# 128x128 squares transposed as two 64-row tiles into two PSUM banks, and scores times values spread over four quarters of TensorE

## The chip, the cores and the metric

The kernel runs on one core of one Trainium2 chip. A core has a matrix engine (TensorE, PE in the profile, with its weight loads listed apart as PEld), VectorE (DVE), ScalarE (ACT), GpSimd (POOL) and SyncE (SP), which here issues the DMAs. The metric is the device time of one execution in microseconds, as the median of several runs of the same program; lower is better.

## The reference, cut to what matters

The kernel computes one encoder block on 16 meta tokens and 1024 tokens of width 1024, all in float32.

```python
h = concat(meta, x)
u = rmsnorm(h)
a, q, k, v, r, lr, ga, gb = split(u @ w_in)
y_a = (pool(a) @ w_pool_mix * pool_scale) @ w_pool_out
# chunks of 64 tokens, 4 heads with keys of 64 and values of 128, b = cumsum(log decay) in a chunk
scores = sum_k q[t,k] * k[s,k] * exp(-|b[t,k] - b[s,k]|)
o  = scores @ v + (q * exp(b)) @ S
S  = exp(b_end) * S + (k * exp(b_end - b)).T @ v
y_b = (rmsnorm(o) * silu(r)) @ w_gla_out
h  = h + (sigmoid(ga) * y_a + sigmoid(gb) * y_b) @ w_out
h  = h + square(relu(rmsnorm(h) @ w_ff1)) @ w_ff2
return rmsnorm(h)[16:]
```

## The kernel before

Features lie on partitions and tokens along the free axis for every product that contracts over the width, so the normalised rows (tokens on partitions) must be transposed first. Every large product is done three times: each operand is split into a high part and a low part (a copy on ScalarE in the type `fp32r`, and a subtraction on VectorE), and `mm3` (L285, L286, L287) issues high×high, high×low and low×high into one accumulation. The two products of the MLP are each one level of a seven-product recursion on halves: `P1` to `P7` for the first (`ff1`), seven products over stored operands for the second (`ff2`).

The stages follow one another: `first` (rows normalised, turned by `turn` at L525, value projection at L285 to L287 in the bank `mm`), the remaining projections, the scores inside chunks (`scores`, L1188), the passes over chunk states (`across`, once for each half of the tokens and each pair `p` of heads), the merge of the two branches (`yb_block`, L1388 to L1393), the output projection (`out_tile`, once for eight tiles of 128 tokens and both column halves; its result leaves PSUM at L1572), the second normalisation with its transposes (`turn_tile`, L1589), then `ff1` and `ff2`.

What sets the order: TensorE's instructions stand in the order in which the program's steps emit them (a manual schedule for that engine). The instructions of ScalarE and VectorE are put in order by a scheduler. Every engine takes its own list strictly in order, and waits at an instruction until the semaphores that it names are there.

PSUM has eight banks of 128 partitions x 512 floats. `banks(keep, tag=n, ...)` closes pools down to `keep` and opens new ones: a tag has `n` buffers used in turn, of one bank each, or of two banks each for the tags that are asked for through `two` (the pairs `sc`, `gs`, `m2`). A buffer that is used again waits for the readers of its former content; a newly opened pool lies over old banks, so its first use of a bank waits for the last readers of what lay there. The pools named in the text are: at the start `sc=1, mm=3, ms=3`; in the passes over states `mm=3, m2=1, ms=1`; from the merge to the second normalisation `mm` kept at 3 and `ms=3`; in most of `ff1` `y=4, z=2` (opened in `ff_room`, `z` for the products P5 and P3).

A square is a 128x128 block of float32 that `pe.transpose` turns: the block is loaded as weights, and `ident`, the unit matrix, is moved through. There are 176: 64 in `first` (eight tiles of tokens, `turn(t, j)` does four squares for j = 0 and four for j = 1, alternating between a bank of `ms` and one of `sc`), 48 in `across` (L1417 turns the decayed keys `kl` into `kt`, L1461 turns the normalised output `on`), 64 in `turn_tile`. In `first`, a turned group of four is read by ScalarE (`keep`, L531, into `xr`; `hi`, L538, into `th`) and VectorE (`lo`, L541, into `tl`). In `turn_tile`, tiles 4 to 7 are read by ScalarE and VectorE to form sums and differences with the tile four before (L1599 to L1605) for the recursion. The last two tiles, 6 and 7, are turned between the first products of `ff1`.

In `across`, the parts of TensorE work on tiles of 64x64 at a `tile_position` (first row, first column of the tile in the array): `kt` times values (L1423) and the queries times states (L1447) use the four quarters in the order (0,0), (1,1), (1,0), (0,1). Scores times values (L1437) uses only the two on the diagonal. The result `o` holds for each head `e` a bank, with the two chunks `u` of a pair on the lower and the upper 64 partitions.

Of the kernel before, what the change touches and what calls it, by code (L numbers as in the profile page):

```python
# [122 lines left out]
def kernel(  # L123
# [25 lines left out]

    banks(sc=1, mm=3, ms=3)  # L150

# [108 lines left out]

    turn_n = [0]

    def transposed(u, half, at, tags=("ms",), to=None):
        rows = u.shape[0]
        th, tl = (t[half] for t in to or (TH, TL))
        if rows == P:
            for j in range(2):
                turn_n[0] += 1
                b = bank(tags[turn_n[0] % len(tags)]).rearrange("p (a b) -> p a b", a=4)
                for i in range(4):  # L270
                    pe.transpose(b[:, i], u[:, (4 * j + i) * P : (4 * j + i + 1) * P], ident)
                split_from_psum(th[:, 4 * j : 4 * j + 4, at : at + P], tl[:, 4 * j : 4 * j + 4, at : at + P], b)
                c = half * HALF + at - OFF[half]
                act.activation(S["xr"][:, 4 * j : 4 * j + 4, c : c + P], b, ACT.Copy)
        else:
            b = bank("ms")[:, : 8 * rows].rearrange("p (a b) -> p a b", a=8)
            for i in range(8):
                pe.transpose(b[:, i], u[:, i * P : (i + 1) * P], ident[:rows, :rows])
            split_from_psum(th[:, :, at : at + rows], tl[:, :, at : at + rows], b)

# [164 lines left out]
    def first_stage(xs, us, xm, um, lrraw):  # L445
# [75 lines left out]
        def turn(t, j):  # L521
            turn_n[0] += 1
            b = turned[t, j] = bank(("ms", "sc")[turn_n[0] % 2]).rearrange("p (a b) -> p a b", a=4)
            for i in range(4):
                pe.transpose(b[:, i], x_out(t)[:, (4 * j + i) * P : (4 * j + i + 1) * P], ident)  # L525

        def kept(t, j):
            return xr[:, 4 * j : 4 * j + 4, t * P : (t + 1) * P]

# [3 lines left out]
        def part(a, t, j):  # L533
            half, at = tok(t)
            return a[half][:, 4 * j : 4 * j + 4, at : at + P]

# [65 lines left out]
    def quad(a):  # L602
        return a.rearrange("p (k c) -> p k c", k=4)
# [571 lines left out]

    def part(i):
        return slice(i * CH, (i + 1) * CH)

    def scores(kk, qq):


        turn_n[0] += 1
        c = (turn_n[0] % 2) * 4 * CH
        b = two("gs")[:, :, c : c + 4 * CH].rearrange("p e (j t) -> p e j t", j=4)
        for j in range(4):
            for e, u in ((0, 0), (1, 1), (1, 0), (0, 1)):
                r, to, s = part(e), part(u), part(2 * j + u)
                pe.matmul(b[to, e, j], kk[r, s], qq[r, s], start=True, stop=True, tile_position=(e * CH, u * CH))  # L1188
        return b
# [90 lines left out]
    def gla_open():  # L1280
# [16 lines left out]
        for half in range(2):  # L1297
# [3 lines left out]
            if half == 0:  # L1301
                ask(6)
        banks(keep=1, mm=3, m2=1, ms=1)

# [99 lines left out]
    def across(p, half):  # L1404
# [9 lines left out]
        sr = S["sr"][p].rearrange("p e t -> p (e t)")  # L1414
        b = quad(bank("ms") if p == 0 else wide2()[:, 0])
        for j in range(4):
            pe.transpose(b[:, j], kl[:, j * P : (j + 1) * P], ident)  # L1417
        act.activation(kt, b, ACT.Copy)
        yield 1.4
        kv = wide2().rearrange("p u (j c) -> p u j c", j=4)  # L1420
        for j in range(4):
            for u, e in ((0, 0), (1, 1), (1, 0), (0, 1)):
                pe.matmul(  # L1423
                    kv[part(e), u, j], kt[part(u), j, part(e)], v[part(u), j, e], start=True, stop=True,
                    tile_position=(u * CH, e * CH),
                )
# [7 lines left out]
        for j in range(4):  # L1434
            for e in range(2):
                for u in range(2):
                    pe.matmul(  # L1437
                        o[part(u), e, j], scc[part(u), e, j], v[part(u), j, e], start=j == 0, stop=False,
                        tile_position=(u * CH, u * CH), skip_group_check=True,
                    )  # L1440

        dve.tensor_copy(rms[p][:, :2], o[:, :, 3, P - 1])
        yield 0.8
        for j in (3, 0, 1, 2):
            for e, u in ((0, 0), (1, 1), (1, 0), (0, 1)):
                c = 2 * j + u
                pe.matmul(  # L1447
                    o[part(u), e, j], qe[part(e), part(c)], states[c][part(e)], start=False, stop=True,
                    tile_position=(e * CH, u * CH), skip_group_check=True,
                )  # L1450
# [7 lines left out]
        yield 8.0  # L1458
        b = wide2().rearrange("p e (j c) -> p (e j) c", j=4)
        for j in range(8):  # L1460
            pe.transpose(b[:, j], on[:, j], ident)  # L1461
        dve.tensor_tensor(sr, b.rearrange("p a c -> p (a c)"), sr, ALU.mult)
        yh, yl = (S["yg"][half][:, n, 2 * p : 2 * p + 2].rearrange("p e t -> p (e t)") for n in range(2))
# [42 lines left out]
    def merge_open():  # L1506
        banks(keep=2, ms=3)
        left.pop_to(left_m)
# [69 lines left out]

    def turn_tile(t, tags=("ms",)):

        u, acc, g = S["u2"][:, ORDER.index(t) % 2], S["acc"], t % 4
        cols, b = slice(g * P, (g + 1) * P), []
        for j in range(2):
            turn_n[0] += 1
            b.append(quad(bank(tags[turn_n[0] % len(tags)])))
            for i in range(4):
                pe.transpose(b[j][:, i], u[:, (4 * j + i) * P : (4 * j + i + 1) * P], ident)  # L1589
        lo, hi = (quad(acc[:, g, c]) for c in halves())  # L1590
        if t < 4:
            for j, raw_copy in enumerate((lo, hi)):
                k = slice(4 * j, 4 * j + 4)
                act.activation(raw_copy, b[j], ACT.Copy)
                split_from_psum(MH[0][:, k, cols], ML[0][:, k, cols], b[j])
# [3 lines left out]
        dve.tensor_tensor(t1, b[0], lo, ALU.subtract)  # L1599
        act.activation(MH[1][:, 0:4, cols], t1, ACT.Copy)  # L1600
        dve.tensor_tensor(ML[1][:, 0:4, cols], t1, f32(MH[1][:, 0:4, cols]), ALU.subtract)  # L1601
        split_from_psum(MH[1][:, 4:8, cols], ML[1][:, 4:8, cols], b[1])
        dve.tensor_tensor(lo, b[1], t1, ALU.subtract)
        dve.tensor_tensor(b12, b[1], b12, ALU.subtract)
        dve.tensor_tensor(hi, hi, lo, ALU.subtract)  # L1605
# [267 lines left out]
    def ff_layers():  # L1873
# [58 lines left out]
```

## Time and profile before

| quantity | value |
|---|---|
| median of 3 runs | 1202.58 us (1202.22 to 1203.32) |
| profiled execution | 1203.16 us |
| span in its profile (first to last instruction) | 1201.4 us |
| TensorE busy | 1187.1 us, 99% of the span |
| VectorE, ScalarE, GpSimd busy | 854.1, 578.7, 101.5 us |
| mean granted TensorE clock | 0.998 |
| 128x128 transposes | 176 matmuls of some 272 ns each, overlapped in the array |

A row of the timeline gives the start in us from the beginning of the span, a duration, the engine, the line, the operation, output<-inputs, and how many records stand together in it; `128*128` is the weight tile and `128x128` the output. TensorE overlaps its matmuls, so how fast it goes is read from the distance between starts, not from the durations. In brackets behind a row stands how long the engine was idle before it and which instruction ended that. A table of stretches (windows) gives the busy time of each engine in each stretch.

### The profile page before, as it was taken

What the parts mean: (1) busy time and instruction counts of PE and PEld (TensorE: products, weight loads), DVE (VectorE), ACT (ScalarE), POOL (GpSimd) and SP (SyncE); (2) the same over time, 40 slices, a digit from 0 to 9 for tenths busy, and PEclk for the clock granted to TensorE, in tenths of its full rate; (3) what the DMA queues carried; (4) which work ended last, traced back from release to release, by engine and by line L of the source; (5) the groups of instructions that cost most, each with busy time, mean ns of one, the idle gap of its engine ahead of it and who ended that gap; (6) DMA issues with size and microseconds to landing.
All of it is one profiled execution on the core that took longest, in us unless ns stands there. A gap on an engine that the chain in (4) does not pass through costs nothing.

```text
span 1201.4 us, 18340 instructions
## 1 busy us (share of the span) xinstructions
PE 1187.1 (99%) x6775; PEld 987.7 (82%) x6775; DVE 854.1 (71%) x1392; ACT 578.7 (48%) x1006; POOL 101.5 (8%) x121
## 2 busy tenths in 40 slices
PE   9999999999999999999999999999999999999997
PEld 7999888777778887888788888888888888888886
DVE  6679557575676669617886767667675887887686
ACT  7566544444455224205754545545454444445554
POOL 0224232333220000000000000000000000000000
PEclk9999999999999999999999999999999999999999
DMA  8232633434358877801264444444389963333532
GB/s 246 68 89 80 182 109 119 144 117 141 124 178 269 304 229 269 268 26 71 88 198 136 158 147 162 148 158 161 128 282 324 336 222 97 97 97 92 172 97 88
DMA packets 151001, 192.79 MB, mean 160 GB/s; under 512 B 12088, under 2 KB 85616, under 8 KB 150912
## 3 DMA queue, kind: packets, MB, share of 16 engines
q1 hardware_dynamic: 150752, 191.56, 49.6%
q8 instruction: 53, 0.87, 0.3%
q14 instruction: 36, 0.29, 0.1%
q10 hardware_dynamic: 160, 0.07, 0.0%
HBM read 128.66 MB, written 62.93 MB: 159 GB/s over the span
## 4 chain that ended last, share of the span: by engine, by line
PE 68%; DVE 3%; issue 1%; DMA 1%; ACT 1%; SPq 0%; DVEq 0%
PE b_oa L287 5%; PE b_oa L286 5%; PE b_oa L285 5%; PE b_y L285 4%; PE b_y L287 4%; PE b_y L286 4%; PE b_mm L285 4%; PE b_mm L287 4%; PE b_mm L286 4%; PE b_ob L287 4%; PE b_ob L286 4%; PE b_ob L285 4%; PE b_z L286 3%; PE b_z L285 3%; PE b_z L287 3%; PE b_sc L285 2%
## 5 line engine op out<-in xcount | busy, mean ns | idle before, releaser
L285 PE MATMUL b_z<-th,w1h 128*128 128x512 f32 x240 | 94.3, 393 | 0.0
L286 PE MATMUL b_z<-tl,w1h 128*128 128x512 f32 x240 | 93.5, 390 | 0.4 <-DVE tl L1601 0.4
L287 PE MATMUL b_z<-th,w1l 128*128 128x512 f32 x240 | 93.5, 390 | 0.0
L285 PE MATMUL b_sc<-th,w1h 128*128 128x512 f32 (+1 forms) x232 | 89.8, 387 | 0.6 <-ACT u2p L1715 0.6
L286 PE MATMUL b_sc<-tl,w1h 128*128 128x512 f32 (+1 forms) x232 | 89.2, 385 | 0.0
L967 ACT ACTIVATE w1h<-raw 128x512 fp32r<-128x512 f32 x103 | 64.0, 622 | 52.4 <-PE b_y L286 23.0
L287 PE MATMUL b_sc<-th,w1l 128*128 128x512 f32 (+1 forms) x232 | 88.9, 383 | 0.0
L967 ACT ACTIVATE w1h<-fs 128x512 fp32r<-128x512 f32 x81 | 51.1, 631 | 66.3 <-PE b_y L286 34.8
L968 DVE TENSOR_TENSOR w1l<-raw,w1h 128x512 fp32r<-128x512 f32 x103 | 70.7, 688 | 15.7 <-ACT w1h L967 15.7
L968 DVE TENSOR_TENSOR w1l<-fs,w1h 128x512 fp32r<-128x512 f32 x81 | 56.2, 693 | 21.6 <-ACT w1h L967 21.6
L967 ACT ACTIVATE w1h<-bt 128x512 fp32r<-128x512 f32 x46 | 29.1, 632 | 70.9 <-issue 43.9
L1791 DVE TENSOR_TENSOR bt<-w,w 128x512 f32<-128x512 f32 x80 | 54.8, 684 | 1.1 <-DMA w<-in_w_ff_dram 1.1
L286 PEld LDWEIGHTS b_z<-tl,w1h 128*128 128x128 f32 x240 | 45.1, 188 | 9.9 <-DVE tl L1601 0.8
L285 PEld LDWEIGHTS b_z<-th,w1h 128*128 128x128 f32 x240 | 45.0, 188 | 9.8 <-issue 0.3
L287 PEld LDWEIGHTS b_z<-th,w1l 128*128 128x128 f32 x240 | 45.1, 188 | 9.7
L285 PEld LDWEIGHTS b_sc<-th,w1h 128*128 128x128 f32 x232 | 43.5, 188 | 10.3 <-ACT u2p L1715 1.1
L287 PEld LDWEIGHTS b_sc<-th,w1l 128*128 128x128 f32 x232 | 43.6, 188 | 8.9
L286 PEld LDWEIGHTS b_sc<-tl,w1h 128*128 128x128 f32 x232 | 43.6, 188 | 8.6
L285 PE MATMUL b_mm<-wo,th 128*128 128x512 f32 x128 | 50.4, 393 | 0.0
L968 DVE TENSOR_TENSOR w1l<-bt,w1h 128x512 fp32r<-128x512 f32 x46 | 31.8, 691 | 25.6 <-ACT w1h L967 25.6
L287 PE MATMUL b_mm<-wo,tl 128*128 128x512 f32 x128 | 49.9, 390 | 0.0
L286 PE MATMUL b_mm<-wo,th 128*128 128x512 f32 x128 | 49.8, 389 | 0.0
(526 smaller groups left out, 3416.3 us busy)
## 6 DMA issues: line engine op xcount, KB each, us to landing
hf_dram<-h SPq DMA_DIRECT2D x112, 256.0 KB, 2.1
raw<-hf_dram SPq DMA_DIRECT2D x112, 256.0 KB, 2.7
w<-in_w_ff_dram SPq DMA_DIRECT2D x64, 256.0 KB, 4.8
raw<-in_w_in_dram SPq DMA_DIRECT2D x18, 512.0 KB, 4.7
raw<-in_w_ff_dram SPq DMA_DIRECT2D x16, 512.0 KB, 4.3
rawx<-in_w_ff_dram SPq DMA_DIRECT2D x16, 512.0 KB, 4.1
rawp<-in_w_in_dram SPq DMA_DIRECT2D x14, 512.0 KB, 4.7
xs<-in_x_dram SPq DMA_DIRECT2D x8, 512.0 KB, 5.2
```

The source lines that it names most:

```text
L285: pe.matmul(ps, ah, bh, start=first and i == 0, stop=False, skip_group_check=more)
L286: pe.matmul(ps, ah, bl, start=False, stop=False, skip_group_check=more)
L287: pe.matmul(ps, al, bh, start=False, stop=last and i == n - 1, skip_group_check=more)
L967: act.activation(hi, a, ACT.Copy)
L968: dve.tensor_tensor(lo, a, f32(hi), ALU.subtract)
L1791: dve.tensor_tensor(bt, w, S["w2"][q[3:]][:, i], ALU.add if q[2] == "+" else ALU.subtract)
```

## The change

`turn_square` replaces one transpose of 128 rows by two transposes of 64 rows: rows 0 to 63 at `tile_position` (0, 0) into the first bank of a pair, rows 64 to 127 at (64, 0) into the second bank, each with 64 columns of `ident`. A square so takes two weight loads of 64x128 and two matmuls of 64 columns, where it took one load of 128x128 and one matmul of 128 columns. 176 loads and 176 matmuls become 352 each. The readers see the pair through `turned_view`, as blocks of 2 x 64 columns. All eight squares of a tile lie in one pair (`sc` and the new `y2` in turn in `first`, `m2` or `sc` in `across`, `m2` in `turn_tile`), so the readers of either group of four lie on the same pair.

In scores times values the second head `e = u ^ to` of each chunk goes to the other half of the rows of the result, so that the product uses all four quarters. The result's halves are swapped for that head, and after the turning L1462's one operation of VectorE becomes three, which swap them back.

To make room for the pairs, the PSUM pools change: at the start `mm=3, ms=1`, with the pair `y2`; in the passes over states `mm=4, m2=1` with no `ms`; in the merge `mm` stays at 4 and `m2=1`; at `wo1_open`, a new set `mm=2, m2=2`.

```diff
-    banks(sc=1, mm=3, ms=3)
+    banks(sc=1, mm=3, ms=1, y2=1)
+    QUARTERS = ((0, 0), (1, 1), (1, 0), (0, 1))
+    def turn_square(pair, k, a):
+        for u in range(2):
+            pe.transpose(pair[:, u, part(k)], a[part(u)], ident[part(u), part(u)], tile_position=(u * CH, 0))
+    def turned_view(pair, n):
+        return pair.rearrange("p u (k s) -> p k u s", s=CH)[:, n]
+    def four(a):
+        return a.rearrange("p k (u s) -> p k u s", s=CH)
...
         def turn(t, j):
-            turn_n[0] += 1
-            b = turned[t, j] = bank(("ms", "sc")[turn_n[0] % 2]).rearrange("p (a b) -> p a b", a=4)
-            for i in range(4):
-                pe.transpose(b[:, i], x_out(t)[:, (4 * j + i) * P : (4 * j + i + 1) * P], ident)
+            if j == 0:
+                turned[t] = two("y2" if t % 2 else "sc")
+            for k in range(4 * j, 4 * j + 4):
+                turn_square(turned[t], k, x_out(t)[:, k * P : (k + 1) * P])
+            turned[t, j] = turned_view(turned[t], slice(4 * j, 4 * j + 4))
...
-        banks(keep=1, mm=3, m2=1, ms=1)
+        banks(keep=1, mm=4, m2=1)
...
-        b = quad(bank("ms") if p == 0 else wide2()[:, 0])
+        b = wide2()
         for j in range(4):
-            pe.transpose(b[:, j], kl[:, j * P : (j + 1) * P], ident)
-        act.activation(kt, b, ACT.Copy)
+            turn_square(b, j, kl[:, j * P : (j + 1) * P])
+        act.activation(four(kt), turned_view(b, slice(0, 4)), ACT.Copy)
...
         for j in range(4):
-            for e in range(2):
-                for u in range(2):
-                    pe.matmul(
-                        o[part(u), e, j], scc[part(u), e, j], v[part(u), j, e], start=j == 0, stop=False,
-                        tile_position=(u * CH, u * CH), skip_group_check=True,
-                    )
+            for u, to in QUARTERS:
+                e = u ^ to
+                pe.matmul(
+                    o[part(to), e, j], scc[part(u), e, j], v[part(u), j, e], start=j == 0, stop=False,
+                    tile_position=(u * CH, to * CH), skip_group_check=True,
+                )
...
-        b = wide2().rearrange("p e (j c) -> p (e j) c", j=4)
+        b = wide2()
         for j in range(8):
-            pe.transpose(b[:, j], on[:, j], ident)
-        dve.tensor_tensor(sr, b.rearrange("p a c -> p (a c)"), sr, ALU.mult)
+            turn_square(b, j, on[:, j])
+        sr8 = four(sr.rearrange("p (a c) -> p a c", c=P))
+        turned = turned_view(b, slice(0, 8))
+        dve.tensor_tensor(sr8[:, :4], turned[:, :4], sr8[:, :4], ALU.mult)
+        for u in range(2):
+            dve.tensor_tensor(sr8[:, 4:, u], turned[:, 4:, 1 - u], sr8[:, 4:, u], ALU.mult)
...
     def merge_open():
-        banks(keep=2, ms=3)
+        banks(keep=2, m2=1)
...
     def wo1_open():
         raw.back()
+        banks(keep=1, mm=2, m2=2)
...
-    def turn_tile(t, tags=("ms",)):
+    def turn_tile(t):
...
+        cols, b, pair = slice(g * P, (g + 1) * P), [], two("m2")
         for j in range(2):
-            turn_n[0] += 1
-            b.append(quad(bank(tags[turn_n[0] % len(tags)])))
-            for i in range(4):
-                pe.transpose(b[j][:, i], u[:, (4 * j + i) * P : (4 * j + i + 1) * P], ident)
+            k = slice(4 * j, 4 * j + 4)
+            for i in range(4 * j, 4 * j + 4):
+                turn_square(pair, i, u[:, i * P : (i + 1) * P])
+            b.append(turned_view(pair, k))
...
-        b12, t1 = (quad(acc[:, t, c]) for c in halves())
-        act.activation(b12, b[0], ACT.Copy)
-        dve.tensor_tensor(t1, b[0], lo, ALU.subtract)
+        b12, t1 = (quad(acc[:, t, c]) for c in halves())
+        act.activation(four(b12), b[0], ACT.Copy)
+        dve.tensor_tensor(four(t1), b[0], four(lo), ALU.subtract)
...
-                turn_tile(ORDER[6 + n // 2], ("mm", "ms"))
+                turn_tile(ORDER[6 + n // 2])
```

The program after is some lines longer: in its listings L525, L1417, L1461 and L1589 are all L270, mm3 is L290 to L292, L1572 is L1580, L1538 is L1545, L1599, L1601, L1603, L1604 are L1606, L1608, L1610, L1611, and L1003, L1669 are L1009, L1676.

First place: TensorE in `first`, about the turning of tile 3, which stands between products of the value projection. Before (`us` is the normalised tile, `vw` the weights):

```order
L287 MATMUL b_mm<-vw_186,tl_136 128x256
L525 MATMUL b_sc<-ident,us 128x128 x4
L525 MATMUL b_ms<-ident,us 128x128 x4
L285 MATMUL b_mm<-vw_186,th_132 128x256
L286 MATMUL b_mm<-vw_186,th_132 128x256
```

and after:

```order
L292 MATMUL b_mm<-vw_189,tl_139 128x256
L270 MATMUL b_y_392<-ident,us 128x64 x16
L290 MATMUL b_mm<-vw_189,th_135 128x256
L291 MATMUL b_mm<-vw_189,th_135 128x256
L292 MATMUL b_mm<-vw_189,tl_139 128x256
```

The block stands at the same place; its eight matmuls into two banks, which came free one by one, are sixteen into the pair `y2` that tile 1 had used.

Second place: VectorE at the opening of the output projection's second part. Before (L1538 makes the low part of the second half of `w_out`, L1572 moves `out_tile`'s result out of PSUM, L968 makes the low parts of the first weights of `ff1`):

```order
L1393 SCALAR_TENSOR_TENSOR tl_144<-o,th_140 128x512
L1538 TENSOR_TENSOR wo_4966<-raw_116,wo_4966 128x1024
L1538 TENSOR_TENSOR wo_4966<-rawx_4962,wo_4966 128x1024
L1572 TENSOR_TENSOR acc<-b_mm,acc 128x512
L1538 TENSOR_TENSOR wo_4966<-raw_120,wo_4966 128x1024
L968 TENSOR_TENSOR w1l<-raw_116,w1h 128x512 x2
L1572 TENSOR_TENSOR acc<-b_mm,acc 128x512
```

and after:

```order
L1396 SCALAR_TENSOR_TENSOR tl_147<-o,th_143 128x512
L1545 TENSOR_TENSOR wo_5090<-raw_119,wo_5090 128x1024
L1545 TENSOR_TENSOR wo_5090<-raw_123,wo_5090 128x1024
L1580 TENSOR_TENSOR acc<-b_mm,acc 128x512
L1545 TENSOR_TENSOR wo_5090<-rawx_5086,wo_5090 128x1024
L974 TENSOR_TENSOR w1l<-raw_119,w1h 128x512 x2
L1580 TENSOR_TENSOR acc<-b_mm,acc 128x512
```

The first L1572 (now L1580) empties the bank of `out_tile(1, 0)` and stands behind two splits of `w_out` in both; the second split is now of `raw_123` instead of `rawx`. What is new is who waits for it: the pool `mm=2` that `wo1_open` opens lies over that bank, so the next tile, `out_tile(2, 0)`, starts behind it.

Third place: VectorE where tile 7 is turned and `ff1` goes on with its first product P5. Before (L968 is a low part of weights, L1609 the low part of a sum):

```order
L968 TENSOR_TENSOR w1l<-fs,w1h 128x512
L1599 TENSOR_TENSOR acc<-b_ms,acc 128x512
L222 TENSOR_TENSOR tl_144<-b_mm,th_140 128x4x128
L1603 TENSOR_TENSOR acc<-b_mm,acc 128x512
L1601 TENSOR_TENSOR tl_144<-acc,th_140 128x4x128
L1604 TENSOR_TENSOR acc<-b_mm,acc 128x512
L1605 TENSOR_TENSOR acc<-acc 128x512
```

and after:

```order
L974 TENSOR_TENSOR w1l<-fs,w1h 128x512
L1606 TENSOR_TENSOR acc<-b_m_5799,acc 128x512
L1009 TENSOR_TENSOR fs<-fs,raw_119 128x512
L1676 TENSOR_TENSOR t4l<-acc,t4h 128x4x128
L1608 TENSOR_TENSOR tl_147<-acc,th_143 128x4x128
L222 TENSOR_TENSOR tl_147<-b_m_5799,th_143 128x4x128
L1610 TENSOR_TENSOR acc<-b_m_5799,acc 128x512
L1611 TENSOR_TENSOR acc<-b_m_5799,acc 128x512
L1612 TENSOR_TENSOR acc<-acc 128x512
```

P5's first matmul waited for the ScalarE half of the split at L222 and its second for L1601. After, its first matmul waits for L1611 too, since the bank `z` that it writes lies over the pair of tile 7, and L1009 and L1676 have come ahead of that.

More of the change, by code (lines that the diff above doesn't have):

```diff
@@ L261, with part, transposed @@
     turn_n = [0]
-    def transposed(u, half, at, tags=("ms",), to=None):
+    QUARTERS = ((0, 0), (1, 1), (1, 0), (0, 1))
+    def part(i):
+        return slice(i * CH, (i + 1) * CH)
+    def turn_square(pair, k, a):
[5 more added lines that the diff above has]
+        return a.rearrange("p k (u s) -> p k u s", s=CH)
+    def transposed(u, half, at, to=None):
         rows = u.shape[0]
         th, tl = (t[half] for t in to or (TH, TL))
-        if rows == P:
-            for j in range(2):
-                turn_n[0] += 1
-                b = bank(tags[turn_n[0] % len(tags)]).rearrange("p (a b) -> p a b", a=4)
-                for i in range(4):
[L271 to L279, printed above, removed]
+        b = bank("ms")[:, : 8 * rows].rearrange("p (a b) -> p a b", a=8)
+        for i in range(8):
+            pe.transpose(b[:, i], u[:, i * P : (i + 1) * P], ident[:rows, :rows])
+        split_from_psum(th[:, :, at : at + rows], tl[:, :, at : at + rows], b)
     def mm3(ps, n, lhs, rhs, first=True, last=True, more=False):
@@ L521, in turn @@
         def turn(t, j):
[L522 to L525 removed]
+            if j == 0:
[3 more added lines that the diff above has]
+            turned[t, j] = turned_view(turned[t], slice(4 * j, 4 * j + 4))
         def kept(t, j):
[L528 removed]
+            return four(xr[:, 4 * j : 4 * j + 4, t * P : (t + 1) * P])
         def keep(t, j):
@@ L534, in part @@
             half, at = tok(t)
-            return a[half][:, 4 * j : 4 * j + 4, at : at + P]
+            return four(a[half][:, 4 * j : 4 * j + 4, at : at + P])
         def hi(t, j):
@@ L1185, in scores @@
         for j in range(4):
-            for e, u in ((0, 0), (1, 1), (1, 0), (0, 1)):
+            for e, u in QUARTERS:
                 r, to, s = part(e), part(u), part(2 * j + u)
@@ L1421, in across @@
         for j in range(4):
-            for u, e in ((0, 0), (1, 1), (1, 0), (0, 1)):
+            for u, e in QUARTERS:
                 pe.matmul(
@@ L1444, in across @@
         for j in (3, 0, 1, 2):
-            for e, u in ((0, 0), (1, 1), (1, 0), (0, 1)):
-                c = 2 * j + u
+            for e, to in QUARTERS:
+                c = 2 * j + (to ^ e)
                 pe.matmul(
-                    o[part(u), e, j], qe[part(e), part(c)], states[c][part(e)], start=False, stop=True,
-                    tile_position=(e * CH, u * CH), skip_group_check=True,
+                    o[part(to), e, j], qe[part(e), part(c)], states[c][part(e)], start=False, stop=True,
+                    tile_position=(e * CH, to * CH), skip_group_check=True,
                 )
@@ L1577, in out_tile @@
         return fn
-    def turn_tile(t, tags=("ms",)):
+    def turn_tile(t):
         u, acc, g = S["u2"][:, ORDER.index(t) % 2], S["acc"], t % 4
-        cols, b = slice(g * P, (g + 1) * P), []
+        cols, b, pair = slice(g * P, (g + 1) * P), [], two("m2")
         for j in range(2):
-            turn_n[0] += 1
-            b.append(quad(bank(tags[turn_n[0] % len(tags)])))
-            for i in range(4):
-                pe.transpose(b[j][:, i], u[:, (4 * j + i) * P : (4 * j + i + 1) * P], ident)
+            k = slice(4 * j, 4 * j + 4)
+            for i in range(4 * j, 4 * j + 4):
+                turn_square(pair, i, u[:, i * P : (i + 1) * P])
+            b.append(turned_view(pair, k))
+        at = lambda a, k=slice(0, 4): four(a[:, k, cols])
         lo, hi = (quad(acc[:, g, c]) for c in halves())
```

12 lines of the change are left out of this document (5 added, 7 removed).

## The prediction

> **What bounds the kernel now.** I read the page's head, the slices and the chain that ended last first, then the stretches, then the places that the change touches row by row.
>
> ```profile
> PE 1187.1 (99%) x6775; PEld 987.7 (82%) x6775; DVE 854.1 (71%) x1392; ACT 578.7 (48%) x1006; POOL 101.5 (8%) x121
> ```
>
> TensorE is busy for all but 14.3 us of 1201.4 us. A nanosecond saved on TensorE is a nanosecond of the total, as long as no other engine is late at that place. Where that fails shows in the stretches (columns: length, PE, PEld, DVE, ACT, POOL busy, clock, DMA share, GB/s):
>
> ```profile
> 10.00:20.00 10.00, 9.54 (x65) 8.46 (x65) 8.72 (x18) 8.37 (x18) 0.00 (x0) 1.00 0.91 265
> 460.00:500.00 40.00, 39.12 (x172) 31.99 (x173) 32.49 (x46) 15.60 (x21) 0.00 (x0) 1.00 0.91 315
> 580.00:600.00 20.00, 18.93 (x89) 15.14 (x88) 18.89 (x34) 14.02 (x27) 0.00 (x0) 1.00 0.25 79
> ```
>
> The granted clock is full. Before 20 us TensorE waits for others and ScalarE and VectorE are busy for over 8 of 10 us, at 460 to 500 us transfers are at 91%, and at 580 to 600 us VectorE is busy for 18.89 of 20. The change frees TensorE mostly elsewhere, but it also alters waits in three of these four stretches.
>
> **What a square costs, before and after.** Before: L1461's sixteen squares of one block, between ordinary matmuls.
>
> ```profile
> 414.44 1.03 PE L1461 MATMUL b_m<-ident,on 128*128 128x128 f32 x8
> 415.31 1.04 PE L1461 MATMUL b_sc<-ident,on 128*128 128x128 f32 x8
> 416.10 0.48 PE L285 MATMUL b_mm<-th,w1h 128*128 128x512 f32 x1
> ```
>
> Eight squares take 415.31 − 414.44 = 0.87 us, 109 ns each, and nothing is lost on entering the block. After, a square is two weight loads of 64x128 and two matmuls of 64 columns at two row positions. No row has just that form; two come near.
>
> ```profile
> 330.67 0.39 PE L287 MATMUL b_y<-t1h,w1l 128*128 128x512 f32 x1
> ...
> 331.51 0.24 PE L1188 MATMUL b_gs<-n 64*64 64x64 f32 x4
> 331.51 0.66 PE L1188 MATMUL b_gs<-n 64*64 64x64 f32 x32
> ...
> 332.43 0.39 PE L286 MATMUL b_z<-tl,w1h 128*128 128x512 f32 x1
> ...
> 55.98 0.26 PEld L278 LDWEIGHTS b_ms<-ident,um 16*128 16x128 f32 x3 [0.15 <-DVE lrtok L406]
> 55.98 0.57 PEld L278 LDWEIGHTS b_ms<-ident,um 16*128 16x128 f32 x8 [0.15 <-DVE lrtok L406]
> ```
>
> The scores move 64 columns through four tiles of 64x64. Their second 32 matmuls, seen first as far as the first four go and then whole, last 0.24 and 0.66 us: seven more groups of four in 0.42 us, 60 ns a group. So four loads and four matmuls of 64 columns, at both row positions and into both banks, share 60 ns. L278 turns the meta rows (16 rows) with loads of full 128 columns: three last 0.26 us and eight 0.57, five more in 0.31, 62 ns each. So I price a new square at 60 to 62 ns instead of 109.
>
> The block of scores also pays for being in tiles. From the last ordinary start ahead of it to the second one behind it are 332.43 − 330.67 = 1.76 us; two ordinary spacings of 0.23 and sixteen groups of 60 ns make 1.42, so 0.34 us is entering and leaving. I take 0.30 to 0.36. A block of eight squares before takes 8 × 109 = 0.88 us; after, 8 × (60 to 62) + (0.30 to 0.36) = 0.78 to 0.86 us, so 0.02 to 0.10 us is won. The one block of sixteen (L1461, first half) wins about 0.4 us. There are 21 blocks: 8 in the first stage, 5 in the passes over states, 8 in the normalisation. Twenty blocks of eight give 0.4 to 2.0 us and the large one 0.4; the first three, in the fed stretch, and the last two, which the wait described below swallows, count for little. I take **−1.4 us**, range −2.4 to −0.6.
>
> [...]
>
> **Scores times values.** Two quarters before, four after; the nearest row is `kt` times values, the same tile, columns and count on four quarters.
>
> ```profile
> 387.30 1.10 PE L1423 MATMUL b_m<-v,kt 64*64 64x128 f32 x32
> 388.22 1.05 PE L1423 MATMUL b_sc<-v,kt 64*64 64x128 f32 x32
> 389.21 0.50 PE L285 MATMUL b_mm<-th,w1h 128*128 128x512 f32 x1
> ...
> 396.27 1.96 PE L1437 MATMUL b_m<-v,gi 64*64 64x128 f32 x32
> 398.07 1.91 PE L1437 MATMUL b_sc<-v,gi 64*64 64x128 f32 x32
> 399.91 0.50 PE L285 MATMUL b_mm<-th,w1h 128*128 128x512 f32 x1
> ```
>
> One block: 399.91 − 396.27 = 3.64 us against 389.21 − 387.30 = 1.91 us, so 1.73 us; it comes twice, once for each half of the tokens, and around it TensorE is busy without a gap: **−3.46 us**. The three multiplies of L1462 instead of one are on VectorE. In the first half the product that needs them comes over 30 us later: nothing. In the second half VectorE is full, and TensorE waits for what stands behind them, the low part of a weight:
>
> ```profile
> 459.83 0.50 PE L287 MATMUL b_mm<-yg,w1l 128*128 128x512 f32 x1
> ...
> 458.55 1.23 DVE L85 TENSOR_TENSOR w1l<-raw,w1h 128x1024 fp32r<-128x1024 f32 x1
> ```
>
> L85 ends at 459.78 and L287 goes on. The three operations move as many columns as the one, so they cost no less; three starts in place of one cost at most twice the 0.60 us at which operations of half the length follow each other (rows of `ff1` below) and by their length more like 0.1 to 0.2. Twice, and with what TensorE is earlier in the two turns there: **+0.3 us**, range 0 to 0.6.
>
> **The banks.** With four `mm` buffers instead of three in the merge, one stall goes:
>
> ```profile
> 474.17 0.50 PE L285 MATMUL b_mm<-yg,w1h 128*128 128x512 f32 x1 [0.88 <-DVE o L1388]
> ```
>
> TensorE idles 0.88 us, and the first matmul after an idle time takes 0.11 longer to the next than usual (0.34 as in the scores' exit, instead of 0.23). The reader of the bank (L1388) now has one more tile's time, about 2.7 us, to come. **−1.0 us**, at worst 0: with TensorE earlier, the next thing late would be the weights' transfers of this stretch (91%).
>
> In the first stage all eight squares of tile 3 go into the pair of tile 1, so they wait for its last copy, where two banks were waited for one by one:
>
> ```profile
> 21.40 0.60 ACT L531 ACTIVATE xr<-b_ms 128x512 f32<-128x512 f32 x1
> 21.57 0.66 PE L525 MATMUL b_sc<-ident,us 128*128 128x128 f32 x4
> ```
>
> The copy ends at 22.00, the block started at 21.57: **+0.45 us**. The matmuls behind it wait too, as TensorE takes its list in order. Later tiles find their pair free.
>
> At `wo1_open` the new `mm` pool lies over the bank of `out_tile(1, 0)`, so `out_tile(2, 0)` waits for L1572 on that bank, which stands on VectorE behind two splits:
>
> ```profile
> 498.82 0.39 PE L285 MATMUL b_mm<-wo,th 128*128 128x512 f32 x1
> ...
> 497.56 1.23 DVE L1538 TENSOR_TENSOR wo<-raw,wo 128x1024 fp32r<-128x1024 f32 x1 [1.18 <-ACT wo L1537]
> 499.79 1.23 DVE L1538 TENSOR_TENSOR wo<-rawx,wo 128x1024 fp32r<-128x1024 f32 x1 [1.00 <-ACT wo L1537]
> 500.93 0.68 DVE L1572 TENSOR_TENSOR acc<-b_mm,acc 128x512 f32<-128x512 f32 x1
> ```
>
> `out_tile(2, 0)` began at 498.82 without a gap. If the two splits run back to back (1.14 us each, 1.23 less the 0.09 us by which such rows overlap: 497.56 + 2.28 = 499.84) and L1572 takes another 0.7, it begins at about 500.58: **+1.76 us**. With L1572 as late as it ran before, to 501.61, it is 2.8; with the splits done early, the move out and its semaphore alone remain, 0.9 (0.7 and a split's rest).
>
> At the first P5 of `ff1`, bank `z` now lies on the pair of tile 7, and the third place of the change shows seven instructions of VectorE to wait for instead of four:
>
> ```profile
> 594.33 0.39 PE L285 MATMUL b_z<-th,w1h 128*128 128x512 f32 x1
> 595.14 0.50 PE L286 MATMUL b_z<-tl,w1h 128*128 128x512 f32 x1 [0.42 <-DVE tl L1601]
> ...
> 592.60 0.69 DVE L1599 TENSOR_TENSOR acc<-b_ms,acc 128x512 f32<-128x512 f32 x1
> ...
> 594.39 0.69 DVE L1601 TENSOR_TENSOR tl<-acc,th 128x512 fp32r<-128x512 f32 x1
> ```
>
> VectorE starts one such instruction every 0.60 us, so seven from 592.60 end at 592.60 + 6 × 0.60 + 0.69 = 596.89; P5 began at 594.33 and lost 0.58 at its second matmul. 596.89 − 594.33 − 0.58 = **+1.98 us**. VectorE has no slack here (18.89 of 20) to catch up; range 0.8 (two of the extra operations fall elsewhere) to 3.0 (two more come ahead).
>
> **The sum.** −1.4 − 3.46 + 0.3 − 1.0 + 0.45 + 1.76 + 1.98 = −1.37 us. Against the profiled execution (1203.16 us, of which 1.76 lies outside the span and is not touched) that is 1201.8; that execution is 0.58 above the median of the runs, so against the median 1202.58 − 1.37 = **1201.2 us**. All lower ends (−2.4, −3.46, 0, −1.0, +0.45, +0.9, +0.8) give −4.7: 1197.9; all upper ones (−0.6, −3.46, +0.6, 0, +0.45, +2.8, +3.0) +2.8: 1205.4. What a measurement of this kernel can tell from no change is about 0.2%, 2.4 us, so 1200.2 to 1205.0 is "same", and the forecast lies inside it, towards the faster side.
>
> **Rivals.**
> - *The new waits are smaller than I read* (they rest on where VectorE's list stands, and TensorE reaches them about 4 us earlier or later than before in a stage where VectorE follows it). The wait at `wo1_open` at 0.9, P5's at 0.8 and squares at 60 ns with 0.30 us a block: −4.7, 1197.9 us; with one of the two waits small, 1199 to 1200. For it: both waits are at most a few VectorE operations long, and VectorE idles 1.18 and 1.00 us just ahead of the two splits. Against: VectorE is full at 580 to 600.
> - *The gain ahead of 500 us is taken back by transfers.* 315 GB/s at 91% in 460 to 500; if the weights there do not come earlier, −3.46 − 1.0 − 0.8 of the squares become waits, and the new ones stay: about +2 to +4, 1204.6 to 1206.6. Against: between 380 and 460 TensorE never waited for a transfer, and the transfers are asked for as buffers come free, which follows TensorE.
> - *The weight loads of the two halves do not overlap* (slower). Place: all 21 blocks. If loads of 128 columns at two row positions go one behind the other, at L278's 62 ns each, a square takes 124 ns instead of 109: 176 × 15 ns + 21 × 0.33 = +9.6 instead of −1.4, sum +9.6: 1212.2. It decides from about 83 ns a square, where the sum passes +2.4. For it: no row has two 128-column loads at two row positions. Against: the scores' four loads share 60 ns, two at each row position.
> - *A load of 128 columns is what sets the 109 ns, whatever its rows.* Then the square stays at 109 ns and only the 21 entries are added: +6.9 for the squares, sum +6.9, 1209.5. Against: L278's loads, 128 columns wide, follow at 62 ns. [...]
>
> **How the numbers follow.** Forecast (within 0.2%) 0.40; smaller waits 0.34; transfers take it back 0.13, of which 0.05 end within 0.2%; loads one behind the other or set by columns 0.13 together. Faster 0.34, same 0.45, slower 0.21. For 8 in 10 the range takes the forecast, the smaller waits and most of the transfers' case: 1197.2 to 1206.0; the forecast's own range is 1200.2 to 1203.5.
>
> **What the profile after would show.** Blocks of sixteen half-squares: a spacing of 60 to 62 ns for each pair, 0.78 to 0.86 us for a block; 109 or more speaks for the last two rivals. L1437's block at 1.9 us, twice. No gap on TensorE near 470 us. New gaps: 0.45 us ahead of the third tile's block at 21 to 22 us, about 1.8 us ahead of the third `wo` tile near 495 us, about 2.6 us ahead of the first `b_z` matmul near 590 us, with VectorE's L1580 and L1611 as what ended them. If those gaps are missing or the ends come from a DMA, the forecast is wrong at that term.

## The result, and the profile after

The changed kernel takes 1212.97 us in the median of four runs (1212.29 to 1215.24), the kernel before 1202.95 us beside it: the ratio is 1.0085, 95% interval 1.0073 to 1.0098, so it is 10.0 us slower. The profiled execution has a span of 1211.5 us. The page's first row and the granted clock in 40 slices:

```profile
PE 1187.4 (98%) x6951; PEld 980.5 (81%) x6951; DVE 854.5 (71%) x1400; ACT 578.7 (48%) x1006; POOL 102.9 (8%) x121
...
PEclk9999999999999999899999999999999999999999
```

The longest waits of TensorE (line, what was waited for; us in total, times, longest):

```profile
PE b_mm L290 <- DVE acc L1580: 5.6, 1, 5.6
PE b_z L290 <- ACT wo L1615: 2.5, 1, 2.5
```

TensorE is idle for 24.1 us instead of 14.3, and two waits that were not there make 8.1 us. That it is busy as long as before hides two things that cancel: with the same squares and products and the clock full throughout it is busy for 1182.4 us (the first experiment below), so what the change saves there is lost again to matmuls at a slower clock. One slice has lost its full clock. Where the time went, by the start of the same instruction in both traces:

| place | before, us | after, us | after − before |
|---|---|---|---|
| last block of scores (L1188) | 351.83 | 354.10 | +2.27 |
| first scores times values (L1437) | 396.27 | 398.50 | +2.23 |
| first queries times states (L1447) | 401.52 | 402.01 | +0.49 |
| second queries times states | 435.47 | 433.99 | −1.48 |
| `out_tile(1, 0)` | 493.38 | 490.92 | −2.46 |
| first turned tile of the normalisation | 545.07 | 551.24 | +6.17 |
| last turned tile | 590.05 | 596.64 | +6.59 |
| last matmul | 1193.26 | 1203.42 | +10.16 |

Up to 491 us the kernel runs 2.5 us ahead of before, although its first stage has lost 2.3. Then one place costs 8.6 us, and one at the start of `ff1` 3.6. The first of them on TensorE and VectorE, and in stretches (length, PE, PEld, DVE, ACT, POOL busy, clock, DMA share, GB/s):

```profile
496.13 0.39 PE L292 MATMUL b_mm<-wo,tl 128*128 128x512 f32 x1
502.15 0.80 PE L290 MATMUL b_mm<-wo,th 128*128 128x512 f32 x1 [5.63 <-DVE acc L1580]
502.74 0.63 PE L291 MATMUL b_mm<-wo,th 128*128 128x512 f32 x1
...
491.85 0.69 DVE L1580 TENSOR_TENSOR acc<-b_mm,acc 128x512 f32<-128x512 f32 x1 [2.14 <-DMA acc<-in_x_dram]
...
499.13 2.36 DVE L1545 TENSOR_TENSOR wo<-raw,wo 128x1024 fp32r<-128x1024 f32 x2 [1.17 <-ACT wo L1544]
501.41 0.68 DVE L1580 TENSOR_TENSOR acc<-b_mm,acc 128x512 f32<-128x512 f32 x1
```

```profile
497.50:500.91 3.41, 0.00 (x0) 0.00 (x0) 2.24 (x3) 2.87 (x3) 0.00 (x0) 1.00 0.52 209
500.91:504.32 3.41, 2.17 (x5) 1.79 (x6) 2.32 (x3) 0.08 (x1) 0.00 (x0) 0.50 0.68 198
504.32:507.74 3.42, 3.42 (x9) 2.65 (x9) 1.29 (x2) 1.15 (x2) 0.00 (x0) 0.50 0.80 262
507.74:511.15 3.41, 3.41 (x16) 2.78 (x16) 0.60 (x1) 1.06 (x1) 0.00 (x0) 1.00 0.00 1
```

The second L1580 is the move out of the bank that `out_tile(2, 0)` needs; TensorE goes on at 502.15, just behind its end (502.09). The first L1580, of the tile before, waited for its rows of x. And when TensorE goes on, it does so at half pace: 427 ns from start to start until 508 us instead of 227, at a granted clock of 0.50 from 500.91 to 507.74 us. The second place is alike:

```profile
600.49 0.39 PE L292 MATMUL b_sc<-th,w1l 128*128 128x512 f32 x1
603.41 0.77 PE L290 MATMUL b_z<-th,w1h 128*128 128x512 f32 x1 [2.53 <-ACT wo L1615]
603.98 0.63 PE L291 MATMUL b_z<-tl,w1h 128*128 128x512 f32 x1
...
602.58 0.68 DVE L1611 TENSOR_TENSOR acc<-b_m,acc 128x512 f32<-128x512 f32 x1
```

The profile names ScalarE's L1615, but VectorE's L1611 ends at 603.26, just ahead; it is the last reader of the pair under `z`. The squares and scores times values themselves, one block of each:

```profile
36.49 0.28 PE L292 MATMUL b_mm<-vw,tl 128*128 128x272 f32 x1
36.70 0.71 PE L270 MATMUL b_y<-ident,us 64*128 64x64 f32 x16
...
37.58 0.29 PE L291 MATMUL b_mm<-vw,th 128*128 128x272 f32 x1
...
398.50 1.10 PE L1440 MATMUL b_m<-v,gi 64*64 64x128 f32 x32
399.42 1.05 PE L1440 MATMUL b_sc<-v,gi 64*64 64x128 f32 x32
400.40 0.50 PE L290 MATMUL b_mm<-th,w1h 128*128 128x512 f32 x1
```

A block of eight squares takes 1.09 us less two ordinary spacings of 0.125, so 0.84 us, and the product 1.90 us instead of 3.64.

### The profile page after: what moved, and what is told of

Its sections match the earlier page's. It is cut to its first block, busy times and chain, and to the rows that moved or that the text cites. A ratio compares the mean times of both kernels' runs of the same rounds, so it can differ in the third digit from the quotient of the medians.

```text
span 1211.5 us, 18691 instructions
## 1 busy us (share of the span) xinstructions
PE 1187.4 (98%) x6951; PEld 980.5 (81%) x6951; DVE 854.5 (71%) x1400; ACT 578.7 (48%) x1006; POOL 102.9 (8%) x121
## 4 chain that ended last, share of the span: by engine, by line
PE 65%; DVE 3%; DMA 3%; issue 1%; ACT 1%; SPq 0%; DVEq 0%; ACTq 0%
PE b_oa L291 5%; PE b_oa L290 5%; PE b_oa L292 5%; PE b_y L290 4%; PE b_y L292 4%; PE b_y L291 4%; PE b_ob L291 4%; PE b_ob L290 4%; PE b_ob L292 4%; PE b_mm L290 3%; PE b_mm L291 3%; PE b_mm L292 3%; PE b_z L290 3%; PE b_z L292 3%; PE b_z L291 3%; PE b_sc L290 2%
## 5 line engine op out<-in xcount | busy, mean ns | idle before, releaser
L290 PE MATMUL b_z<-th,w1h 128*128 128x512 f32 x240 | 95.3, 397 | 2.5 <-ACT wo L1615 2.5
L292 PE MATMUL b_z<-th,w1l 128*128 128x512 f32 x240 | 94.0, 392 | 0.0
L290 PE MATMUL b_sc<-th,w1h 128*128 128x512 f32 (+1 forms) x232 | 89.8, 387 | 0.9 <-ACT u2p L1722 0.9
L292 PE MATMUL b_sc<-th,w1l 128*128 128x512 f32 (+1 forms) x232 | 88.9, 383 | 0.0
L290 PE MATMUL b_mm<-wo,th 128*128 128x512 f32 x128 | 51.8, 405 | 5.6 <-DVE acc L1580 5.6
L290 PEld LDWEIGHTS b_z<-th,w1h 128*128 128x128 f32 x240 | 45.4, 189 | 13.0 <-ACT wo L1615 2.9
L292 PEld LDWEIGHTS b_z<-th,w1l 128*128 128x128 f32 x240 | 45.4, 189 | 9.9
L290 PEld LDWEIGHTS b_sc<-th,w1h 128*128 128x128 f32 x232 | 43.5, 188 | 10.4 <-ACT u2p L1722 1.2
L292 PE MATMUL b_mm<-wo,tl 128*128 128x512 f32 x128 | 50.8, 397 | 0.0
L292 PEld LDWEIGHTS b_sc<-th,w1l 128*128 128x128 f32 x232 | 43.6, 188 | 8.8
```

The lines of the kernel that those rows point to most:

```text
L290: pe.matmul(ps, ah, bh, start=first and i == 0, stop=False, skip_group_check=more)
L292: pe.matmul(ps, al, bh, start=False, stop=last and i == n - 1, skip_group_check=more)
```

## Experiments: the two waits, the first stage, the product alone

The theory was: two waits for reused banks, a slow clock behind each, and a first stage that has lost its even pace; the squares are harmless. The rivals: a cost of the squares wherever TensorE goes from whole tiles to tiles of 64 rows and back (their mode changes), and transfers that would take the time whatever the banks are. Four kernels tell them apart.

**The pools at `wo1_open` in the other order.**

```diff
-        banks(keep=1, mm=2, m2=2)
+        banks(keep=1, m2=2, mm=2)
```

> The changed kernel with the pool of pairs opened ahead of the pool mm at wo1_open, so that mm lies over the two banks of the old pair and the pairs over the four old mm banks; later z lies over mm instead of over the last turned pair. Theory (two bank waits and a lowered clock after each): the stall at out_tile(2, 0), 5.8 us and 3.1 us of half clock behind it, and the one at the first P5, 2.7 us and 1.6 us, both go, apart from the 0.6 us that P5 lost before: 1213.0 - 8.9 - 3.6 = about 1200.5 us, and the clock shows no dip near 500 and 603 us. Rival (the squares and their mode changes cost the time, spread over 21 blocks): no more than 1 us gained, about 1212. Rival (late transfers of the x rows stop TensorE anyway, one tile later): half of it comes back as a stall at out_tile(3, 0) or (4, 0), about 1206.

Measured: 1201.13 us (11 runs), before 1202.46 us (18 runs); ratio 0.9989, 0.9980 to 0.9997. The order of two names is worth 11.8 us against the changed kernel (11.5 by the two ratios). No stall moves to a later tile: between 485 and 505 us TensorE is busy throughout, at full clock, though VectorE still waits for rows of x.

```profile
490.00:495.00 5.00, 5.00 (x24) 4.13 (x23) 3.85 (x6) 0.98 (x2) 0.00 (x0) 1.00 1.02 375
495.00:500.00 5.00, 5.00 (x24) 4.14 (x23) 3.50 (x4) 3.25 (x4) 0.00 (x0) 1.00 0.58 223
...
489.90 0.69 DVE L1580 TENSOR_TENSOR acc<-b_mm,acc 128x512 f32<-128x512 f32 x1 [1.87 <-DMA acc<-in_x_dram]
```

So the squares were not the cause, and the transfers are late without holding TensorE, as long as no bank ties it to them.

**The first stage as before.**

```diff
-    banks(sc=1, mm=3, ms=1, y2=1)
+    banks(sc=1, mm=3, ms=3)
...
+            b = bank(("ms", "sc")[turn_n[0] % 2]).rearrange("p (a b) -> p a b", a=4)
+            for i in range(4):
+                pe.transpose(b[:, i], x_out(t)[:, (4 * j + i) * P : (4 * j + i + 1) * P], ident)
+            turned[t, j] = four(b)
```

> The changed kernel with the first stage as before (128x128 squares, banks sc=1, mm=3, ms=3), all else as changed. Theory (the first 80 us lost 2.6 us to waits for banks and for ScalarE, not to the squares): about 1210.4 us, and everything behind 80 us moves by that much. Rival (the 2.6 us are the start of one profiled run, with its slower first matmuls): 1 us or less, 1212 to 1213.

Measured: 1208.54 us (1204.95 to 1210.34); ratio 1.0046, 1.0033 to 1.0059: 4.4 us gained. In the profiles the stretch from 20 to 80 us tells it, first of the changed kernel, then of this one:

```profile
20.00:80.00 60.00, 58.10 (x515) 54.52 (x515) 45.34 (x65) 39.78 (x80) 9.80 (x11) 1.00 0.34 96
```

```profile
20.00:80.00 60.00, 59.98 (x486) 57.54 (x486) 47.13 (x68) 41.76 (x84) 12.15 (x12) 1.00 0.35 96
```

TensorE lost 1.9 us there, 1.6 of it at three places of the changed kernel:

```profile
22.51 0.71 PE L270 MATMUL b_y<-ident,us 64*128 64x64 f32 x16 [0.26 <-ACT xr L537]
50.81 0.58 PE L270 MATMUL b_y<-ident,us 64*128 64x64 f32 x12 [0.60 <-DVE small L509]
66.58 0.39 PE L290 MATMUL b_mm<-vw,th 128*128 128x272 f32 x1 [0.76 <-ACT vo L416]
```

The two profiled executions lie 5.2 us apart: 1.9 here, 2.2 by a shorter stall at `out_tile(2, 0)` (3.4 us), which the next group takes up, and 1.1 by fewer matmuls at half pace behind it. On ScalarE, from 9 to 80 us, the changed kernel has a wait that neither this one nor the kernel before has (line, what was waited for; us in total, times, longest):

```profile
ACT th L544 <- DVE tl L547: 5.4, 5, 1.9
```

ScalarE's high part of one group of four waits for VectorE's low part of the other. Both groups lie in one pair of banks now, and lay in a bank each before. It is a likely reason why ScalarE and VectorE are late at the second and third of the places above; the shared pair is not tested apart from the half squares.

**Scores times values alone**, on the kernel before.

```diff
-            for e in range(2):
-                for u in range(2):
+            for u, to in ((0, 0), (1, 1), (1, 0), (0, 1)):
+                e = u ^ to
...
-        dve.tensor_tensor(sr, b.rearrange("p a c -> p (a c)"), sr, ALU.mult)
+        dve.tensor_tensor(sr8[:, :4], b8[:, :4], sr8[:, :4], ALU.mult)
+        for u in range(2):
+            dve.tensor_tensor(sr8[:, 4:, u], b8[:, 4:, 1 - u], sr8[:, 4:, u], ALU.mult)
```

> The kernel before with scores times values alone changed (all four quarters, and three multiplies on VectorE instead of one); squares and pools as before. Theory (3.46 us of TensorE are won at 396 and 431 us and nothing behind takes them back): 1202.9 - 3.3 = about 1199.6 us. Rival (the transfers between 460 and 500 us take the gain back): 1202 to 1203, with a new gap on TensorE ahead of 500 us.

Measured: 1198.81 us, ratio 0.9970 (0.9959 to 0.9982): 3.65 us gained. The product gives what its rows promised, and nothing takes it back.

**Both mended**: the other pool order and the first stage as before.

> The changed kernel with the pools at wo1_open in the other order and the first stage as before. Theory: 1213.0 - 8.9 - 3.6 - 2.6 = about 1198 us, clearly faster than before. Rival (the turned squares in the passes and in the normalisation win nothing, only scores times values does): as that change alone, 1199.6. Rival (transfers): above 1202.

Measured: 1197.99 us (1197.58 to 1198.51), ratio 0.9963 (0.9951 to 0.9975). This beats both kernels. Against the product alone it is 0.8 us less, within their intervals. Against the other pool order alone (1201.13 us) the first stage as before is worth 3.1 us.

## Experiments: how long the stalls are, and the clock

**The x rows asked for earlier**, in the changed kernel.

```diff
     for k in range(4):
         step(rest, load_wo(0, k))
+    step(rest, lambda: x_again(0, 1))
     yb(3)
     yb(0)
-    step(rest, lambda: x_again(0, 1))
     step(rest, out_tile(0, 0))
```

> The changed kernel with the x rows of the first two output tiles asked for ahead of yb(3) instead of after yb(0), all else as changed. Theory (the stall at out_tile(2, 0) is that long because VectorE's L1580 of out_tile(0, 0) waits until 491.85 us for its x rows, and the chain behind it on VectorE and ScalarE leads to the bank): L1580 runs at about 489.7, the stall shrinks from 5.8 to about 3.7 us, the slow clock behind it with it, 1213.0 - 2.1 - 1.1 = about 1209.8 us. Rival (the order on VectorE and the weights' transfers alone set the stall): the stall stays between 5.3 and 6 us, 1212 to 1213.

Measured: 1207.67 us, with a wide spread (1205.19 to 1212.47); ratio 1.0045, 1.0028 to 1.0063, below the changed kernel's interval. L1580 no longer waits for x:

```profile
490.06 0.69 DVE L1580 TENSOR_TENSOR acc<-b_mm,acc 128x512 f32<-128x512 f32 x1
...
488.25 0.69 DVE L1391 SCALAR_TENSOR_TENSOR t<-t,b_mm 128x512 f32<-128x512 f32 x1 [1.86 <-DMA t<-gb_dram]
```

The stall is 3.2 us instead of 5.6. But the next thing late is a transfer too (`t` from `gb_dram`), and TensorE came 1.5 us later than in the changed kernel for other reasons in this execution, so only 1.0 us of it is an earlier bank (free at 501.10 instead of 502.09). That the transfers set the chain's start is shown; the share of the x rows alone is not. The spread goes with the clock: the two fastest executions (1205.2 and 1205.4 us) have a mean granted clock of 0.999 and 0.998, the two slowest (1211.3 and 1212.5) 0.995 and 0.994.

**`z` over the mm banks**, in the changed kernel.

```diff
-        banks(keep=1, y=4, z=2)
+        banks(keep=1, z=2, y=4)
```

> The changed kernel with z opened ahead of y in ff_room, so that z lies over the two mm banks and y over the pairs; the stall at out_tile(2, 0) stays. Theory: P5 waits as before the change, which gives back 2.7 - 0.6 us of stall and 1.6 us of half clock: 1213.0 - 3.7 = about 1209.3 us. Rival (VectorE's and ScalarE's work there holds TensorE at the next product anyway): less than 1.5 us, with a new wait on b_y or b_z by 606 us.

Measured: 1210.81 us, ratio 1.0068 (1.0055 to 1.0080): 2.2 us gained where I expected 3.7. The stall at P5 is gone with its slow stretch. But `ff2` lays its first banks over `z` in this order, and a new wait came there:

```profile
893.97 0.47 PE L290 MATMUL b_oa<-w1h 128*128 128x512 f32 x1 [1.77 <-DVE h L1750]
```

3.6 us at P5 less 1.8 leaves 1.8, near the 2.2 measured. In the kernels with the pools of `wo1_open` swapped, `z` stays where it was and this wait does not arise.

This run has the changed kernel's program up to P5, and its stall at `out_tile(2, 0)` was 3.7 us. From the start of the first L1580 to TensorE's restart it is 10.3 us in each: 491.85 to 502.15 in the changed kernel, here 489.71 to 500.02, with the first stage as before 487.43 to 497.74. The chain behind it (two tiles of the merge, ScalarE's and VectorE's splits of `w_out`, the move out) has the same length in all three. Its start differs by 2.1 us between the first two, whose programs are alike up to there, while `out_tile(1, 0)` starts at 490.92 and 490.68: TensorE's arrival does not move with it.

**Stalls put into the kernel before**, first by VectorE and then shorter ones by ScalarE, to see the clock alone.

```diff
             b, n = bank("mm"), ORDER.index(t)
+            for _ in range({(4, 0): 2, (6, 0): 5, (2, 1): 11}.get((t, ch), 0)):
+                prev = ORDER[n - 1] if ch else t - 1
+                dve.tensor_copy(b, S["acc"][:, prev, ch * HALF : (ch + 1) * HALF])
```

> The kernel before with three stalls put in: ahead of out_tile(4, 0), (6, 0) and (2, 1) VectorE first writes 2, 5 and 11 copies of the tile before into the bank, 0.6 us each, so that TensorE should idle for about 1.9, 3.7 and 7.3 us (the result of those tiles is not changed). Theory (an idle TensorE loses its clock after some 2 to 3 us and runs at half of it for about as long as it idled): full pace at once after the first, half pace for about 3.5 us after the second and 6 to 7 us after the third, 12.9 + 1.8 + 3.5 = 18 us longer, 1221. Rival (the slow stretches of the changed kernel came from transfers or chance): 227 ns from start to start right after every idle time, 13 us longer, 1215 to 1216.

```diff
+            for _ in range({(3, 0): 1, (5, 0): 2, (7, 0): 3, (2, 1): 4}.get((t, ch), 0)):
+                prev = ORDER[n - 1] if ch else t - 1
+                act.activation(b, S["acc"][:, prev, ch * HALF : (ch + 1) * HALF], ACT.Copy)
```

> The kernel before with four short stalls: ahead of out_tile(3, 0), (5, 0), (7, 0) and (2, 1) ScalarE writes 1, 2, 3 and 4 copies of the tile before into the bank (the results are not changed); TensorE should idle for about 1.4, 2.0, 2.6 and 3.2 us. Theory (the clock falls once the idle time passes a bound between 1.1 and 2.7 us, and then for 3 to 6 us whatever its length): full pace after 1.4 us and half pace after 2.6 and 3.2; 2.0 us tells on which side the bound lies. Rival (any idle time costs clock in proportion): a slow stretch of 1 to 2 us already after the first.

Measured: 1230.64 and 1218.42 us, one run each. The idle times came out longer than planned, since the copies stood behind other work: 5.4, 4.4 and 12.5 us, and 2.1, 2.1, 2.7 and 7.0. The first and the last of them in the first kernel, then three of the second:

```profile
514.14 0.77 PE L285 MATMUL b_mm<-wo,th 128*128 128x512 f32 x1 [5.44 <-DVE b_mm L1566]
514.71 0.63 PE L286 MATMUL b_mm<-wo,th 128*128 128x512 f32 x1
...
579.94 0.80 PE L285 MATMUL b_mm<-wo,th 128*128 128x512 f32 x1 [12.46 <-DVE b_mm L1566]
580.53 0.63 PE L286 MATMUL b_mm<-wo,th 128*128 128x512 f32 x1
```

```profile
505.30 0.50 PE L285 MATMUL b_mm<-wo,th 128*128 128x512 f32 x1 [2.09 <-ACT b_mm L1566]
505.64 0.39 PE L286 MATMUL b_mm<-wo,th 128*128 128x512 f32 x1
...
532.40 0.50 PE L285 MATMUL b_mm<-wo,th 128*128 128x512 f32 x1 [2.68 <-ACT b_mm L1566]
532.74 0.40 PE L286 MATMUL b_mm<-wo,th 128*128 128x512 f32 x1
...
568.67 0.80 PE L285 MATMUL b_mm<-wo,th 128*128 128x512 f32 x1 [6.96 <-ACT b_mm L1566]
569.27 0.63 PE L286 MATMUL b_mm<-wo,th 128*128 128x512 f32 x1
```

In these rows the first spacing behind an idle time is 0.34 us at full pace and 0.57 to 0.60 at half. So far the theory holds: the clock fell behind idle times that were put in, with no transfer in them. That it stays low for about as long as TensorE idled is wrong: 7 matmuls at 427 ns follow 4.4, 5.4 and 7.0 us of idling, 12 follow 12.5 us, and in the changed kernel 12 follow 5.63 and 7 follow 2.53. Nor does the length of the idle time alone decide: 2.53 us cost the clock, 2.68 us did not. In the changed kernel the granted clock is half for 6.83 us at the first stall (500.91 to 507.74 us) and for 3.41 us at P5 (603.31 to 606.72). Two stretches about P5's stall in the changed kernel, and two about the 2.68 us of the short stalls (behind the length stands TensorE's busy time, third from the end the clock):

```profile
599.90:603.31 3.41, 0.98 (x5) 0.48 (x3) 3.41 (x7) 2.04 (x5) 0.00 (x0) 1.00 0.00 0
603.31:606.72 3.41, 3.31 (x8) 2.66 (x9) 3.41 (x6) 1.22 (x3) 0.00 (x0) 0.50 0.00 0
```

```profile
527.59:531.00 3.41, 2.13 (x10) 1.43 (x8) 0.69 (x1) 0.52 (x1) 0.00 (x0) 1.00 0.00 0
531.00:534.41 3.41, 2.01 (x9) 1.68 (x10) 0.00 (x0) 1.28 (x3) 0.00 (x0) 1.00 0.00 0
```

At P5 the clock is half from 603.31 us, 0.10 us ahead of TensorE's restart; about the 2.68 us it stays full. What decides beside the length of the idle time is not shown.

**The normalisation's squares whole again**, in two steps on the mended kernel: first only the transposes, then also without the new pools at `wo1_open` (four banks `mm` and two `ms` from the merge on).

```diff
-                turn_square(pair, i, u[:, i * P : (i + 1) * P])
-            b.append(turned_view(pair, k))
+                pe.transpose(quad(pair[:, j])[:, i % 4], u[:, i * P : (i + 1) * P], ident)
+            b.append(four(quad(pair[:, j])))
```

> The changed kernel with both pool orders mended and the first stage as before, and the 64 squares of the normalisation turned whole again (128x128, into the two banks of a pair); only the passes keep half squares. Theory (a block of eight half squares wins 0.03 us there and the later waits for small cost 0.3 us twice): 1198.0 - 0.3, 1197.7 us, not to be told from it. Rival (half squares win 0.1 us a block in the normalisation): 1198.8.

```diff
-        banks(keep=2, m2=1)
+        banks(keep=2, ms=2)
...
-        banks(keep=1, m2=2, mm=2)
...
+            whole = quad(bank(tags[turn_n[0] % len(tags)]))
+            for i in range(4):
+                pe.transpose(whole[:, i], u[:, (4 * j + i) * P : (4 * j + i + 1) * P], ident)
```

> The mended kernel with half squares and four mm buffers kept only in the passes and the merge: first stage as before, no new pools at wo1_open, and the normalisation with whole squares in the two banks of ms (the last two tiles in mm and ms, as before the change). Theory (half squares win about 0.07 us a block of eight, but the two waits for the row statistics in the normalisation, 0.3 us each, came with the new pools): no waits for small there, 1198.0 - 0.1 to 0.5, about 1197.7 us. Rival (two banks of ms instead of three hold up the turning): a wait on b_ms in each block, above 1199.

Measured: 1198.48 us (ratio 0.9967, 0.9955 to 0.9979) and 1197.52 us (ratio 0.9956, 0.9942 to 0.9969). By time the three mended kernels are the same. The traces part them: from the first turned tile to the last it is 45.40 us with half squares and 45.94 with whole ones. A block that nothing holds up wins 0.04 us by half squares (6.30 and 6.33 us from one block to the next instead of 6.33 and 6.37); the rest lies at two waits of 0.3 us for the row statistics (`small`, L255), which both kernels have. Without the new pools these two waits are gone, and it is 44.98 with whole squares.

## Why the prediction was wrong

I forecast 1201.2 us, no change that can be told, and the kernel takes 1213.0. By the steps of the sum:

- **The squares' price was right.** Behind the first pair of a block the pairs follow at 60 to 65 ns, a little over the 60 to 62 given, and a block of eight takes 0.84 us, where 0.78 to 0.86 was given. What they win, 0.04 us a block of eight in the normalisation, lies in the range of 0.02 to 0.10. The two rivals on the weight loads are out; that one of them named 1212.2 us is an accident.
- **Scores times values was right:** −1.74 us at each block in the table, −3.65 us for the change alone.
- **The merge was right:** from the second queries times states to `out_tile(1, 0)` it gains 0.98 us. The stall at 474 us is gone, and the wait for L85 at 460 us grew by 0.3.
- **The first stage was mis-sized:** +2.27 us against the +0.45 of tile 3's wait less a few tenths. Tile 3's wait came as priced (TensorE lost 0.43 us there). Missed were two later waits: at 50.81 for VectorE, which ends the normalised rows of tile 7 (L515) at 50.75 (the profile names the small operation behind it), and at 66.58 for ScalarE, where a copy of a bank had come behind a conversion of 1.92 us. The 0.7 us at the very start are no part of it, since they differ from execution to execution: the first block of squares starts between 9.95 and 11.06 us with the first stage as before and between 10.45 and 11.37 with the changed one. From there to the last block of scores it is 343.1 us in each of the four traces with the changed stage, and 340.6 to 341.5 in the eight others, of which the trace of before is the longest. So the stage costs 2.0 to 2.5 us against the other seven, not 0.45.
- **The wait at `wo1_open` is the step that failed:** +1.76 us, range to 2.8, measured +8.63. I took all times of VectorE's chain from the trace of before, as if TensorE came there when it came before, or as if the chain came earlier with it. With before's numbers the formula holds: L1572 at 490.24 plus 10.3 is 500.5. But TensorE came 2.5 us earlier, by the gains that I had counted, and the chain 1.6 us later, by the rows of x. A wait on something that transfers pace grows by what TensorE gains ahead of it, less what the transfers come earlier with it. With scores times values alone changed they did so in part: TensorE came 4.5 us earlier than in the trace of before, the chain 3.3. I had that as a rival (transfers take the gain back) and as a range, but did not add the two. 1.76 + 2.46 + 1.61 gives 5.8 us of stall. How late the chain comes is in part the execution: with `z` over the mm banks, alike up to there, the chain came 0.5 us earlier than before and TensorE 2.7, and 1.76 + 2.70 − 0.53 = 3.9 us is what TensorE lost there (it went on at 500.02 instead of 496.12).
- **The clock was left out altogether:** the other 2.8 us there, and 1.7 at P5, are matmuls at half pace behind the stalls. The trace of before holds no idle time of TensorE over 0.9 us behind the first stage, its granted clock is 1.00 from 20 to 1193 us, and so shows none of it.
- **P5's wait was right, its price was not:** by the shift of the last turned tile, L1611 was to end at 596.89 + 6.59 = 603.48, and it ended at 603.26. The stall of 2.53 us less before's 0.42 is near the 1.98 us given; the total is +3.57 with the slow clock.
- **The rival of smaller waits**, given 0.34, had nothing to make the waits smaller: of the two pauses of VectorE ahead of the splits the second did go, but the sum had that already.

## What to carry to other kernels

A pool that is opened over old banks ties its first user to the last reader of what lay there (here L1580 ends at 502.09 us and TensorE goes on at 502.15): of two pools that are opened together, lay the one that is used at once over the banks that have been quiet longest (worth 11.8 us here). Price such a wait as the distance of two arrivals, and shift each of them by what the change does to it; an engine that is made faster can run into waits on transfers that were hidden, as TensorE did here when it came 2.5 us earlier. And an idle time of TensorE can cost more than its length, for the clock behind it: in the changed kernel 2.8 us more behind 5.63 us of idling and 1.7 us more behind 2.53, while behind the 2.1 us that were put in the pace was full at once.

## What the runs showed of the hardware

- After idle times of TensorE of 3.2 us and more (3.2 to 12.5 us, in six kernels) the clock fell to half each time (427 instead of 227 ns from start to start for 7 or 12 matmuls, 3.0 or 5.1 us), after 2.1 us it did not, in either of two cases, and of 2.53 us (P5's stall, in three kernels) and 2.68 us the shorter one cost it.
- In the changed kernel pairs of loads of 64x128 weights at two row positions, with their matmuls of 64 columns, follow at 60 to 65 ns a pair, while one such load is listed with 138 ns: they overlap. So a load of 128 columns does not hold a square at 109 ns.
